# Attention scores of two components, issued in turn on the two halves of TensorE's rows

## The chip, the cores and the metric

The kernel runs on one core of one Trainium2 chip. The metric is the device time of one execution in microseconds (us); of three runs of the kernel before, the median is 1934.57 us (1925.41 to 1936.29).

## The reference

A backbone of two layers for 512 latent tokens and 256 context tokens of 1024 channels. Each layer has a modulated RMS norm, one input projection whose columns feed three groups of heads (a long convolution, a gated unit, differential attention), an output projection, and a SwiGLU feed-forward part. The change is in the differential attention alone: four heads, each with two components of 64 channels, whose softmaxes are subtracted:

```
s = einsum('bqhcd,bkhcd->bhcqk', q, k) * (DA_HEAD_DIM ** -0.5)
a = softmax(s, axis=-1)
w = a[:, :, 0] - lam * a[:, :, 1]
o = einsum('bhqk,bkhd->bqhd', w, v)
```

Latent queries attend to all 256 context keys and all 512 latent keys in one softmax. Context tokens attend to the 256 context keys, in layer 0 only, since nothing reads their result in layer 1.

## The kernel before, in words

All of TensorE's large products are computed from split operands: each float32 value is a high part of 12 bits and the exact rest, and a product is three matmuls, high by high, high by low and low by high. `mm3` (line 245) issues the three, on lines 251, 252 and 253, for every product in the kernel, so most of TensorE's time stands on these three lines; what a row is for is read from its shape. Scores are the only products on 64 rows whose output has 128 rows and comes from these lines.

`attend` (line 654) takes two heads. For each half of the query tokens, each head and each tile of 128 queries it computes the scores of component 0 and then of component 1. A head's 128 channels lie on the 128 partitions: component 0 on partitions 0 to 63, component 1 on 64 to 127, and so on the two halves of the array's rows. For a latent tile a component has 768 score columns, 512 latent and 256 context ones, in two PSUM banks: three matmuls of 512 columns, then three of 256. For a context tile it has 256 columns in one bank. After each component VectorE takes the row maximum (line 683) and scales it (line 686), and ScalarE takes the exponential out of PSUM and its sum (line 688). When both components have theirs, VectorE forms the weighted difference (lines 692 to 694). After two tiles the weights are transposed on TensorE (line 703), split, and multiplied with the values. There are 16 latent tiles in a layer and 8 context tiles.

PSUM has eight banks, which one arena hands out, the longest unused first (`Arena.get`, line 62). Scores take theirs from the group S, banks 2 to 5, by `ps` (line 219); the gated unit, the convolution and the filter spectra use the same group for some steps, and the latent stream's projections use S and A.

The work is written as generators, one per task: the latent stream, the context stream, the filter spectra and the modulation weights. `woven` (line 167) runs several side by side. Each step of a generator adds its matmul time to `self.cost` (columns / 2400 for each matmul), and the generator whose sum over its rate is lowest goes next; a step counts as at least 1. In `lat_mixer` (line 1416) the first pair of heads is woven with the gated unit and the projections of the second pair (line 1433), and the second pair with the output projection and the norm that follows it (lines 1442 to 1448). The order of issue is the priority with which a planner then puts each instruction on its engine's queue: an instruction whose operands or whose memory are not due yet by its plan lets later ones of other tasks go ahead. Each engine takes its queue in that order, and instructions wait there for semaphores.

Of the kernel before, what the change touches and what calls it, by code (L numbers as in the profile page):

```python
# [38 lines left out]
class Buf:  # L39
    """A piece of an arena; emit-time lifetime, slices like a tile."""  # L40
# [11 lines left out]
class Arena:  # L52
    """Blocks of one tile, handed out longest-unused first, so that reuse waits little."""
# [8 lines left out]
    def get(self, shape, allowed=None):  # L62
# [9 lines left out]
        for p in range(0, self.units - u + 1, step):  # L72
            if allowed is not None and p not in allowed:
                continue
            if any(self.used[p:p + u]):
                continue
            blk = p // 4 * 4
            whole = u < 4 and not any(self.used[blk:blk + 4])
            key = (whole and allowed is None, max(self.stamp[p:p + u]))
            if best is None or key < best[0]:  # L80
                best = (key, p)
# [12 lines left out]
    def fits(self, sizes):  # L94
        """Whether blocks of these units can be had, one beside the other."""
        used = list(self.used)
        for u in sorted(sizes, reverse=True):
            step = 4 if u > 2 else u
            p = next((p for p in range(0, self.units - u + 1, step) if not any(used[p:p + u])), None)
            if p is None:  # L100
                return False
            used[p:p + u] = [True] * u
        return True
# [9 lines left out]
class Stream:  # L113
    """One token stream (latent or context) in channel-major form."""
# [10 lines left out]
# PSUM banks by use, arena sizes in KiB per partition.  # L125
BANKS = {"A": (0, 1, 6, 7), "S": (2, 3, 4, 5), "W": (6, 7), "P": (6, 7)}
UNITS = {"R": 104, "RW": 24, "F": 44, "FW": 24}
# Rates of the tasks in each phase (the latent stream has 10), and of the woven steps of each layer.
# [5 lines left out]
# Work of the latent and of the context stream that GpSimd does ("mix": 2 is all of it, 1 a half).  # L134
# [8 lines left out]
# Steps of the tasks that come first, the chunks of modulation weights that are fetched ahead, and  # L143
# the arenas of the weights of the first feed-forward tiles.
# [5 lines left out]
class Net:  # L150
# [16 lines left out]
    def woven(self, *tasks):  # L167
        """Generators (gen, rate) side by side; the matrix work of each grows at its rate.

        A rate may be a key of self.rates, which change with the phases."""  # L170
# [20 lines left out]
    def room(self, *sizes):  # L191
        """Waits until the float32 arena has room for the next step."""
        while not self.F.fits(sizes):
            yield "wait"

    def claim(self, n):
        """Waits until n units of the operand arena are spoken for by nobody."""
# [25 lines left out]
    def tt(self, n, dtype=F32):  # L223
        """Tiny per-partition scratch, round robin."""
# [5 lines left out]
    def split(self, src, hi, lo, lo_eng=None):  # L230
        """hi = src rounded to 12 bits, lo = the rest, exactly."""
# [3 lines left out]
    def weights(self, src, *shape, pool=False, arena=None):  # L235
        """A split piece of weights of this shape; the low part by GpSimd if pool."""
# [8 lines left out]
    def mm3(self, out, terms):  # L245
        """out = sum of lhsT^T rhs over split terms: hi hi + hi lo + lo hi."""
# [9 lines left out]
    def rsqrt(self, ms, n, out=None):  # L256
        """1/sqrt by an exponent guess and three Newton steps."""
# [12 lines left out]
    def rstd_bcast(self, sq, T, n, groups="P", scale=None):  # L270
        """sq [P, T]: squares per channel row; PSUM [P, T] with 1/rms per token in every row.

        With scale [P, T / P] the channels are scale times the values that are meant: the result
        normalizes the values and takes the factor out."""
# [52 lines left out]
    def lambdas(self):  # L327
        """The weights of the second softmax, and the gains that follow."""
# [18 lines left out]
    def rope_tables(self, l):  # L347
        """Rotation tables of q and k with the norm gains folded in."""
# [10 lines left out]
    def ada_load(self, l, c, arena):  # L359
        """A chunk of modulation weights, as it is, in two pieces."""  # L360
# [6 lines left out]
    def ada(self, l, secs, groups="P", ready=(), own="W"):  # L367
        """Modulation sections; mods[l][:, s*8+k, v] is channel k*128+p of section s for stream v."""
# [60 lines left out]
    def x_open(self, st, a):  # L429
        """Channel tiles 2a and 2a+1 of x, resident or fetched from the home of the stream."""  # L430
# [12 lines left out]
    def pairs(self, n, T):  # L443
        """n split operands of [P, T]."""
        return [Pair.one(self.r(2, T)) for _ in range(n)]

    def square(self, st, k, x, cols=slice(None)):
        """Adds the squares of x, channel tile k, to the running sum; k in order."""
# [10 lines left out]
    def norm(self, st, l, w, cols=slice(None), squares=True, early=None):  # L459
        """st.h = split(rmsnorm(x) * G + shift), channel-major."""  # L460
# [37 lines left out]
    def modulate(self, st, l, w, k, y, cols):  # L498
        """y * G + shift in y's place and its high part; gives what makes the low part."""
# [15 lines left out]
    def proj_cm(self, st, l, n, out):  # L515
        """out [P, T]: the n-th 128 output channels of the input projection by tokens."""
# [4 lines left out]
    def proj_tm(self, st, w, tt, out):  # L521
        """out [P, 256]: one token tile by the chunk's 256 output channels."""
# [3 lines left out]
    def pool(self, st, i):  # L526
        """Whether GpSimd does this part of the stream's work."""
        return POOL[i][st.v]

    def win(self, st, l, c):  # L530
        """Weights of 256 output channels, in two pieces along the input channels."""
        return [self.weights(self.A["w_in_tm"][l, c - 4, :, 4 * i:4 * i + 4], 4, CW, pool=i and self.pool(st, "in tm")) for i in range(2)]

# [1 line left out]
    def qk(self, st, l, c, i, rope):  # L535
        """Two heads of q (i=0) or k (i=1): projection, norm per 64 channels, rotation;
        split [(component channel), tokens] per head."""
# [60 lines left out]
    def vproj(self, st, l, c):  # L598
        """Two heads of v, token-major: per two token tiles a split [P, 2, 256]."""
# [13 lines left out]
    def kqv(self, st, l, j, rope, q=True):  # L613
        """Keys, queries and values of heads 2j and 2j+1."""
# [27 lines left out]
    def kv_io(self, st, j, mem, store):  # L642
        """Keys and values of a head pair of a context-sized stream to or from DRAM scratch."""
# [9 lines left out]

    def attend(self, st, l, j, srcs):
        """Heads 2j and 2j+1 of stream st over the keys and values of srcs."""
# [8 lines left out]
        for qh in range(0, st.nt, 2):  # L664
# [3 lines left out]
            for h in range(2):  # L668
                q = st.q[j][h]
                ws = []  # L670
                for qt in (qh, qh + 1):
                    yield from self.room(e, e, 2)
                    i0 = 2 * h + qt - qh
                    es, sums = [], [s0[:, i0:i0 + 1], self.tt(1)]
                    for c in range(2):
                        b = self.ps("S", nk)
                        r = slice(c * HD, (c + 1) * HD)
                        off = 0
                        for s in reversed(srcs):
                            self.mm3(b[:, off:off + s.T], [(q[r, qt * P:(qt + 1) * P], s.k[j][h][r, :])])  # L680
                            off += s.T
                        m = self.tt(1)
                        nc.vector.tensor_reduce(m, b.ap, axis=AX.X, op=ALU.max)  # L683
# [4 lines left out]
                        nc.scalar.activation(es[c].ap, b.ap, AF.Exp, bias=m, scale=scale,  # L688
                                             accum_out=sums[c])
                        b.free()  # L690
# [115 lines left out]
    def sin_reduced(self, out, z, n):  # L806
        """out = sin(z) for any moderate z: z - 2 pi round(z / 2 pi) in three parts, then the table."""
# [22 lines left out]
    def dft(self, out, tab, cs, ft, data, n):  # L830
        """out[f, ch] = sum over tokens (one parity) of tab[token, f] * data[token, ch]."""
# [3 lines left out]
    def filters(self, groups="S"):  # L835
        """Hidden features of the filter networks: rows 64 l + channel, columns SEQ | CTX positions."""
# [33 lines left out]
    def spectra(self, l, L, dst, groups="S"):  # L870
        """Filter spectra of layer l at length L, scaled by 1/L, to DRAM scratch."""
# [76 lines left out]
    def short_conv(self, st, l, c, split_par):  # L948
        """Width-3 convolution of one 256-channel chunk; even|odd token order where asked."""
# [25 lines left out]
    def to_tokens(self, src, par, n, groups):  # L975
        """PSUM [P, n, 256]: one parity of [ch, even|odd tokens] with tokens on partitions."""
# [7 lines left out]
    def fwd(self, data, tabs, kdram, o, L, groups):  # L984
        """Spectral product of token-major data (per parity, split [P, n, 256]) with a filter.

        Gives split operands: even tokens take (cos, sin) = (a, c), odd tokens (b, d), each [P, n, 256]."""
# [140 lines left out]
    def outproj(self, st, l, ks, last=False):  # L1128
        """x += gate1 * (w_out[ks rows]^T mix[ks])."""
# [29 lines left out]
    def outproj_last(self, st, l, ks, parts):  # L1159
        """The last rows of the output projection, all columns, in parts of the tokens."""  # L1160
# [28 lines left out]
    def hidden(self, st, w, a, cols):  # L1189
        """a = split(silu(g) * u) for one tile of FFN channels and a range of tokens."""  # L1190
# [19 lines left out]
    def ffn(self, sts, l, rounds, ahead=(), last=False, ready=None):  # L1210
        """The feed-forward part of the streams, which share the weights.

        The first tiles, their weights in the arenas of ahead, take the tokens of the first stream
        in halves; only after them the other streams have to be ready."""
# [63 lines left out]
class Pair:  # L1278
    """Split operand: indexing gives the same piece of hi and lo."""
# [20 lines left out]
class Columns:  # L1300
    """Split weights [2, P, k, 128] of two tiles of output channels, in one piece or two.

    The second piece is fetched when the first is; a piece goes when it is done, unless on hold."""
# [259 lines left out]
def _layout(i):  # L1563
    """The inputs, only moved: transposed, cut into tiles, repeated."""
# [55 lines left out]
```

## Time and profile before

| | |
|---|---|
| median of 3 runs (lowest to highest) | 1934.57 us (1925.41 to 1936.29) |
| span of the profiled execution | 1924.6 us |
| the run nearest to that span | 1925.41 us |
| TensorE busy (matmul, weight load) | 1813.6 us, 1558.6 us |
| VectorE, ScalarE, GpSimd busy | 1082.6, 689.1, 119.7 us |
| granted TensorE clock, mean | 0.968 |

The span runs from the first to the last instruction of the core. PE is TensorE's matmuls, PEld its weight loads, DVE VectorE, ACT ScalarE, POOL GpSimd. Matmuls are pipelined: a row's start is when it began, its duration reaches into the next matmul's, so the pace is read from start to start. The granted clock is a share of full speed; the engine has two levels, 1.2 and 2.4 GHz.

### The profile page before, as it was taken

The numbers are of one execution on the slowest core, as the hardware profiler recorded it, in microseconds if no ns is written. First come the engines' busy times: TensorE is split into PE (matmuls) and PEld (weight loads), VectorE is DVE, ScalarE is ACT, GpSimd is POOL, SyncE is SP. The second block draws the span as 40 slices with busy tenths as digits, with TensorE's granted clock in tenths as the row PEclk, the third lists the DMA queues.
The fourth block names the chain that finished last, engine by engine and source line by source line (L and its number), as shares of the span: only waits on it lengthen the run. The fifth ranks groups of instructions, "written<-read, shape, count | busy, mean of one in ns | idle before, by whom it ended". The sixth has DMA issues, their size and how long they took to land.

```text
span 1924.6 us, 27933 instructions
## 1 busy us (share of the span) xinstructions
PE 1813.6 (94%) x11106; PEld 1558.6 (81%) x11106; DVE 1082.6 (56%) x2255; ACT 689.1 (36%) x1203; POOL 119.7 (6%) x128
## 2 busy tenths in 40 slices
PE   5799999789997999999999999899999999999999
PEld 2578898678776888888888888689988788888887
DVE  5677886778767523232423244789588773333333
ACT  2544434544544421212122112543455462222221
POOL 1100223211001000000000000011000000000000
PEclk9899899799997999999999999899999899999999
DMA  7567644235444343243424234444213222323231
GB/s 272 177 233 237 201 162 143 83 125 187 134 167 147 111 126 127 84 136 108 144 83 151 74 102 156 153 154 144 79 34 119 64 71 63 110 84 105 89 97 64
DMA packets 89564, 245.41 MB, mean 128 GB/s; under 512 B 9780, under 2 KB 21782, under 8 KB 89434
## 3 DMA queue, kind: packets, MB, share of 16 engines
q1 hardware_dynamic: 81162, 221.71, 35.2%
q0 software_dynamic: 8272, 21.92, 3.8%
q8 instruction: 87, 1.43, 0.3%
q14 instruction: 43, 0.35, 0.1%
HBM read 221.18 MB, written 22.41 MB: 127 GB/s over the span
## 4 chain that ended last, share of the span: by engine, by line
PE 79%; DVE 9%; DMA 4%; ACT 3%; issue 2%; POOL 0%; SPq 0%; ACTq 0%; DVEq 0%; POOLq 0%
PE banks L251 25%; PE banks L252 24%; PE banks L253 24%; PE banks L401 2%; PE banks L703 1%; DMA x_ctx<-F 1%; DVE RW L233 1%; DMA F<-x_ctx 1%; ACT F L688 1%; DVE tiny L683 1%; DVE F L1025 1%; PE banks L375 1%; PE banks L279 1%; DVE F L456 1%; DMA FW<-in_w_out 0%
## 5 line engine op out<-in xcount | busy, mean ns | idle before, releaser
L251 PE MATMUL banks<-R,RW 128*128 128x512 f32 (+1 forms) x1984 | 696.0, 352 | 9.1 <-ACT R L504 3.9
L252 PE MATMUL banks<-R,RW 128*128 128x512 f32 (+1 forms) x1984 | 693.9, 350 | 3.0 <-DVE R L507 3.0
L253 PE MATMUL banks<-R,RW 128*128 128x512 f32 (+1 forms) x1984 | 692.2, 349 | 0.5 <-DVE RW L233 0.5
L232 ACT ACTIVATE RW<-FW 128x1024 fp32r<-128x1024 f32 (+2 forms) x240 | 240.5, 1003 | 541.4 <-PE banks L252 418.9
L251 PEld LDWEIGHTS banks<-R,RW 128*128 128x128 f32 x1984 | 376.9, 190 | 64.7 <-ACT R L504 4.7
L252 PEld LDWEIGHTS banks<-R,RW 128*128 128x128 f32 x1984 | 377.0, 190 | 51.4 <-DVE R L507 3.8
L253 PEld LDWEIGHTS banks<-R,RW 128*128 128x128 f32 x1984 | 376.7, 190 | 50.4 <-issue 2.0
L233 DVE TENSOR_TENSOR RW<-FW,RW 128x1024 fp32r<-128x1024 f32 (+2 forms) x228 | 262.7, 1154 | 238.0 <-ACT RW L232 229.4
L1186 DVE SCALAR_TENSOR_TENSOR F<-banks,mods,F 128x512 f32<-128x512 f32 (+1 forms) x192 | 116.2, 615 | 177.4 <-PE banks L253 133.8
L251 PE MATMUL banks<-R 128*128 128x256 f32 (+3 forms) x584 | 188.0, 340 | 26.4 <-ACT R L1036 13.7
L252 PE MATMUL banks<-RW,R 128*128 128x256 f32 x624 | 180.0, 289 | 5.4 <-DVE RW L233 5.4
L251 PE MATMUL banks<-RW,R 128*128 128x256 f32 x624 | 181.1, 291 | 0.4 <-ACT F L552 0.2
L252 PE MATMUL banks<-R 128*128 128x256 f32 (+3 forms) x584 | 179.6, 319 | 1.4 <-DVE R L233 1.4
L253 PE MATMUL banks<-RW,R 128*128 128x256 f32 x624 | 180.2, 289 | 0.0
L253 PE MATMUL banks<-R 128*128 128x256 f32 (+3 forms) x584 | 177.5, 315 | 1.2 <-DVE R L1038 1.2
L251 PEld LDWEIGHTS banks<-R 128*128 128x128 f32 (+1 forms) x584 | 117.4, 209 | 49.6 <-ACT R L1036 15.2
L1204 DVE TENSOR_TENSOR F<-F,banks 128x256 f32<-128x256 f32 (+1 forms) x71 | 40.0, 565 | 208.5 <-PE banks L253 191.8
L232 ACT ACTIVATE R<-F 128x512 fp32r<-128x512 f32 (+1 forms) x133 | 72.0, 549 | 226.9 <-DVE F L1204 160.9
L252 PEld LDWEIGHTS banks<-R 128*128 128x128 f32 (+1 forms) x584 | 119.8, 209 | 10.0 <-issue 3.5
L252 PEld LDWEIGHTS banks<-RW,R 128*128 128x128 f32 x624 | 121.7, 195 | 7.6 <-DVE RW L233 6.3
L251 PEld LDWEIGHTS banks<-RW,R 128*128 128x128 f32 x624 | 121.5, 195 | 3.1 <-ACT F L552 0.8
L253 PEld LDWEIGHTS banks<-RW,R 128*128 128x128 f32 x624 | 121.8, 195 | 2.2 <-issue 1.5
(159 smaller groups left out, 1739.7 us busy)
## 6 DMA issues: line engine op xcount, KB each, us to landing
FW<-in_ffn_w SPq DMA_DIRECT2D x104, 512.0 KB, 3.7
FW<-in_ada_w SPq DMA_DIRECT2D x96, 512.0 KB, 5.0
FW<-in_w_in_tm SPq DMA_DIRECT2D x50, 512.0 KB, 4.8
R<-in_tab POOLq DMA_DIRECT2D x28, 512.0 KB, 4.9
FW<-in_w_in_cm SPq DMA_DIRECT2D x24, 512.0 KB, 4.7
F<-x_ctx SPq DMA_DIRECT2D x36, 256.0 KB, 3.6
FW<-in_ffn_w SPq DMA_DIRECT2D x24, 384.0 KB, 2.9
x_ctx<-F SPq DMA_DIRECT2D x32, 256.0 KB, 2.4
```

The lines of the kernel that those rows point to most:

```text
L232: self.nc.scalar.activation(hi, src, AF.Copy)
L233: (lo_eng or self.nc.vector).tensor_tensor(lo, src, hi.bitcast(F32), op=ALU.subtract)
L251: mm(out, lhsT=lh, rhs=rh, start=(i == 0), stop=False)
L252: mm(out, lhsT=lh, rhs=rl, start=False, stop=False)
L253: mm(out, lhsT=ll, rhs=rh, start=False, stop=(i == n - 1))
L279: nc.tensor.matmul(p1[:, t:t + 1], lhsT=sq[:, t * P:(t + 1) * P], rhs=self.ones[:, 0:1], start=True, stop=True)
L375: nc.tensor.matmul(pt[:, b], lhsT=sb[:, b // 2, b % 2 * P:(b % 2 + 1) * P], rhs=self.pick, start=True, stop=True)
L401: nc.tensor.matmul(pa[32 * j:32 * j + 32, :], lhsT=self.cv[:, 4 * i + j, :], rhs=w[:, j, :], start=(i == 0), stop=(i == 1), tile_position= ...
L456: nc.vector.tensor_tensor(st.acc[:, cols], st.acc[:, cols], q.ap, op=ALU.add)
L683: nc.vector.tensor_reduce(m, b.ap, axis=AX.X, op=ALU.max)
L1186: self.nc.vector.scalar_tensor_tensor(x, p, self.mods[l][:, sec * 8 + k, st.v:st.v + 1], x, op0=ALU.mult, op1=ALU.add)
L1204: nc.vector.tensor_tensor(s.ap, s.ap, u, op=ALU.mult)
```

## The change

`attend` takes one buffer for both components of a tile: four banks, always banks 2 to 5, for a latent tile, and two banks of group S for a context tile. A new function `scores` issues the matmuls of both components in turn: component 0 high by high, component 1 high by high, component 0 high by low, and so on, for the 512 latent columns and then for the 256 context columns. Maximum and exponential follow component by component as before, and the buffer is given back after both exponentials. `scores` adds 3 x columns / 2400 to `self.cost` once for both components. `Arena.get` gets an argument for a fixed place. The diff also empties comments and docstrings; this generates nothing and is left out here.

```
-    def get(self, shape, allowed=None):
+    def get(self, shape, allowed=None, at=None):
...
-        for p in range(0, self.units - u + 1, step):
+        for p in range(0, self.units - u + 1, step) if at is None else (at,):
...
+    def score_banks(self, nk):
+        if nk <= 512:
+            return self.B.get([P, 2, 512], set(BANKS["S"]))
+        return self.B.get([P, 2, 1024], at=BANKS["S"][0])
+
+    def scores(self, b, off, q, k, n):
+        (qh, ql), (kh, kl) = q, k[:, :]
+        self.cost += 3 * n / 2400
+        for i, (x, y) in enumerate(((qh, kh), (qh, kl), (ql, kh))):
+            for c in range(2):
+                r = slice(c * HD, (c + 1) * HD)
+                self.nc.tensor.matmul(b[:, c, off:off + n], lhsT=x[r], rhs=y[r], start=(i == 0), stop=(i == 2))
...
+                    b = self.score_banks(nk)
+                    off = 0
+                    for s in reversed(srcs):
+                        self.scores(b, off, q[:, qt * P:(qt + 1) * P], s.k[j][h], s.T)
+                        off += s.T
                     for c in range(2):
-                        b = self.ps("S", nk)
-                        r = slice(c * HD, (c + 1) * HD)
-                        off = 0
-                        for s in reversed(srcs):
-                            self.mm3(b[:, off:off + s.T], [(q[r, qt * P:(qt + 1) * P], s.k[j][h][r, :])])
-                            off += s.T
                         m = self.tt(1)
-                        nc.vector.tensor_reduce(m, b.ap, axis=AX.X, op=ALU.max)
+                        nc.vector.tensor_reduce(m, b[:, c, :nk], axis=AX.X, op=ALU.max)
...
-                        nc.scalar.activation(es[c].ap, b.ap, AF.Exp, bias=m, scale=scale,
+                        nc.scalar.activation(es[c].ap, b[:, c, :nk], AF.Exp, bias=m, scale=scale,
                                              accum_out=sums[c])
-                        b.free()
+                    b.free()
```

## Rows read from the trace of the kernel before

**Rows 1.** The page, parts 1 and 4: busy time, share, count; chain by engine.

```profile
PE 1813.6 (94%) x11106; PEld 1558.6 (81%) x11106; DVE 1082.6 (56%) x2255; ACT 689.1 (36%) x1203; POOL 119.7 (6%) x128
...
PE 79%; DVE 9%; DMA 4%; ACT 3%; issue 2%; POOL 0%; SPq 0%; ACTq 0%; DVEq 0%; POOLq 0%
```

**Rows 2.** Busy time by stretch: length, each engine (instructions), clock, DMA share, GB/s.

```profile
350.00:430.00 80.00, 67.30 (x413) 58.00 (x413) 61.31 (x138) 40.52 (x74) 18.35 (x14) 0.83 0.27 86
495.00:590.00 95.00, 86.50 (x554) 67.12 (x553) 67.34 (x156) 48.01 (x97) 0.57 (x1) 0.92 0.47 153
1378.00:1445.00 67.00, 66.89 (x451) 58.18 (x449) 57.08 (x145) 36.11 (x65) 0.00 (x0) 0.97 0.12 38
1445.00:1545.00 100.00, 93.39 (x531) 76.88 (x529) 80.24 (x200) 52.67 (x99) 1.65 (x3) 0.93 0.30 94
```

**Rows 3.** TensorE's timeline, 1436.0 to 1437.4: start, duration, line, shape.

```profile
1436.08 0.49 PE L251 MATMUL banks<-R 64*128 64x512 f32 x1
1436.41 0.39 PE L252 MATMUL banks<-R 64*128 64x512 f32 x1
1436.64 0.39 PE L253 MATMUL banks<-R 64*128 64x512 f32 x1
1436.87 0.28 PE L251 MATMUL banks<-R 64*128 64x256 f32 x1
1436.99 0.28 PE L252 MATMUL banks<-R 64*128 64x256 f32 x1
1437.11 0.28 PE L253 MATMUL banks<-R 64*128 64x256 f32 x1
1437.32 0.38 PE L253 MATMUL banks<-RW,R 128*128 128x256 f32 x1
```

**Rows 4.** TensorE's timeline, 1513.5 to 1515.5 (x2: two rows merged).

```profile
1513.57 0.49 PE L251 MATMUL banks<-R 64*128 64x512 f32 x1
...
1514.14 0.39 PE L253 MATMUL banks<-R 64*128 64x512 f32 x1
1514.15 0.51 PE L251 MATMUL banks<-R 64*128 64x512 f32 x2
...
1515.19 0.28 PE L253 MATMUL banks<-R 64*128 64x256 f32 x1
1515.40 0.39 PE L251 MATMUL banks<-R,RW 128*128 128x256 f32 x1
```

**Rows 5.** TensorE's timeline, 1462.5 to 1464.1.

```profile
1462.58 0.51 PE L251 MATMUL banks<-R 64*128 64x512 f32 x2
1462.92 0.40 PE L252 MATMUL banks<-R 64*128 64x512 f32 x2
...
1463.99 0.50 PE L251 MATMUL banks<-R,RW 128*128 128x512 f32 x1
```

**Rows 6.** TensorE's timeline, starts of two runs of twelve score matmuls.

```profile
351.74 0.79 PE L251 MATMUL banks<-R 64*128 64x512 f32 x1
...
1526.01 0.50 PE L251 MATMUL banks<-R 64*128 64x512 f32 x1 [2.52 <-ACT F L688]
```

**Rows 7.** The timeline of all engines, 1384.5 to 1386.7.

```profile
1384.58 0.99 ACT L688 ACTIVATE F<-banks,tiny,rq 128x768 f32<-128x768 f32 x1
...
1385.56 0.98 ACT L688 ACTIVATE F<-banks,tiny,rq 128x768 f32<-128x768 f32 x1
...
1386.68 0.50 PE L251 MATMUL banks<-R 64*128 64x512 f32 x1
```

**Rows 8.** VectorE's groups, 1378 to 1445: count, busy us, mean ns, idle before.

```profile
L683 DVE TENSOR_REDUCE tiny<-banks 128x1 f32<-128x768 f32 x16 | 15.2, 952 | 4.1 <-PE banks L253 4.1
L694 DVE SCALAR_TENSOR_TENSOR F<-F,tiny 128x768 f32<-128x768 f32 x7 | 7.1, 1013 | 0.0
...
L233 DVE TENSOR_TENSOR R<-banks,R 128x512 fp32r<-128x512 f32 x8 | 5.3, 686 | 1.9 <-ACT R L232 1.9
```

**Rows 9.** TensorE's waits, 350 to 430 and 1445 to 1545: total, times, longest.

```profile
PE banks L251 <- ACT F L688: 5.3, 2, 4.0
...
PE banks L251 <- ACT F L688: 2.5, 1, 2.5
```

## The prediction

> **What bounds the kernel now.** The order of reading was: the page's busy times and its chain of waits, then the busy time of each engine in the four stretches in which the latent stream attends, then TensorE's own timeline inside them, then its waits. TensorE is busy 94% of the span and carries 79% of the chain that ends last [rows 1], so a microsecond taken from its queue is worth most of a microsecond, as long as something else stands ready for it. The four attention stretches are less even [rows 2]. At 1378 to 1445 TensorE is busy 66.89 of 67 us, at 1445 to 1545 it is idle for 6.6 us, at 495 to 590 for 8.5 us, at 350 to 430 for 12.7 us, with a granted clock there of 0.83, that is, a third of the stretch at the lower of the two levels. VectorE is busy 77%, 71%, 85% and 80% of the four, in order of time. So TensorE sets the pace in one stretch of four, and in the others the softmax chain does so for part of the time.
>
> What the change touches is 32 latent tiles of scores (16 a layer), each two components of six matmuls on 64 rows: three of 512 columns and three of 256. TensorE's timeline shows three ways in which such a tile runs now. A component by itself takes 1437.32 - 1436.08 = 1.24 us [rows 3], so a tile whose components stand apart costs 2.48 us. Where the two components follow each other, the tile takes 1515.40 - 1513.57 = 1.83 us [rows 4]: the second component's first matmul (1514.15) starts 0.01 us after the third of the first component, while three of the first are still to come, and from there on the two run side by side on the two halves of the rows. In one tile both first matmuls start together and it takes 1463.99 - 1462.58 = 1.41 us [rows 5]. So the overlap that the change asks for is there already in part. Going through the timeline, the latent matmuls form fourteen unbroken runs of twelve with both halves (the first at 351.74, the last at 1526.01 [rows 6]), seven of them at 1.83 to 1.85 us; the rest, the equal of 18 tiles, is broken by work of other tasks or by waits.
>
> **The change part by part.** *Alternating order.* Nothing is added or removed: the same twelve matmuls and twelve weight loads a tile. Fully paired, a tile costs what one component costs now plus the step between the halves, an estimate of 1.24 + 0.01 = 1.25 us, or 1.41 us by the nearest row [rows 3, 5]; I take 1.25. An unbroken run then saves 1.83 - 1.25 = 0.58 us, a broken tile up to 2.48 - 1.25 = 1.23 us. The ceiling is 14 x 0.58 + 18 x 1.23 = 30.3 us, the floor nothing.
>
> Which tiles will pair? The planner puts an instruction on TensorE's queue when its operands and its bank are due. The first component's banks come free with its exponential, the second's 0.98 us later (1385.56 against 1384.58, and the next scores start only after them, at 1386.68) [rows 7]. A tile whose first component is due earlier will go on being issued first component first, whatever order the code has. So I let the fourteen unbroken runs pair, and 2 of the 18 broken ones. Of the fourteen, two stand in the stretch where TensorE is full and count whole; four at 1445 to 1545 and six at 495 to 590 count by half, since the idle time there shows that a TensorE that is earlier often waits for the softmax; two at 350 to 430 count nothing. That is 2 + 5 = 7 x 0.58 = 4.1 us, and 2 x 1.23 = 2.5 us for the broken ones. What comes late next is VectorE: its row maxima, weighted differences and low parts of the attention are 15.2 + 7.1 + 5.3 us of the full stretch [rows 8].
>
> That row stands beside a rule of the Trainium skill, TensorEngine Tiling (Array Packing), section PSUM Bottleneck: tiling speeds up the matmuls but not the emptying of PSUM, which can become the limit. Were it so in all four stretches the 4.1 us would be nothing; the trace agrees for three of them and not for 1378 to 1445, where TensorE has 0.1 us to spare and VectorE 9.9 us.
>
> *Context tiles* (8 in layer 0, three pairs of 256 columns): 24 matmuls on either half at 0.12 us from start to start (1436.99 - 1436.87 [rows 3]) are 2.9 us that could go beside the other half; I take 1 us, between nothing and 2.9.
>
> *The four-bank buffer.* Before, two components in two banks each also filled the four score banks, so the depth is the same. It adds no instruction. What it can add is a wait: the second matmul of a tile now belongs to the second component. Bounds: nothing, where both halves are free; 0.98 us a tile where the planner's order is ahead of the real exponentials [rows 7]. I take nothing, because TensorE's waits for the exponential are few now: 5.3 us in two waits and 2.5 us in one [rows 9], and the last of them, at 1526.01 [rows 6], holds up a first component, which either order does.
>
> *The weave.* The step of a latent tile was booked at 2 x 3 x 768 / 2400 = 1.92 and is now 0.96, which the weaver counts as 1. A head's two tiles and its product with the values were 3 x 1.92 = 5.76 and become 3.92, so beside one head's softmax stands 3.92 / 5.76 = 0.68 of the other tasks' matmuls. The softmax has the same work in less cover, and the uncovered matmuls run later, where TensorE is full. The price is idle TensorE. Bounds: if all stretches fell to the idle share of 350 to 430 (15.9%), the other three would lose 95 x 0.159 - 8.5 = 6.6, 67 x 0.159 - 0.1 = 10.6 and 100 x 0.159 - 6.6 = 9.3, together 26.5 us; in the other direction a new weave could at best fill the 27.9 us that are idle now [rows 2]. I take the one step that I can see coming: the full stretch falls to the idle share of the last one, 67 x 0.066 = 4.4 us lost.
>
> **Sum.** 4.1 + 2.5 + 1.0 - 4.4 = 3.2 us less. The profiled span is 1924.6 us and the nearest run 1925.41, 0.8 us around it: 1922.2 by that execution. It stands 9.2 us below the median of the three runs, 1934.57; on the median the forecast is 1931.4 us.
>
> **The rivals.** *All tiles pair.* For it: the code gives both components as one block, and halves that are both due can run as at 1462.58 [rows 5]. Against: the staggered release of the banks. Price: with the same shares (whole in the full stretch, half elsewhere), about two thirds of 30.3, 20 us less: 1915 us.
>
> The Trainium skill's page TensorE: Matmul & The Clock Gate, section The mechanism, has matmuls start and end in the order of the program, with no reordering. By that rule only an alternating order can pair, and what the change gives is near this rival's. The start at 1514.15 [rows 4] does not go with it, unless the planner had already mixed the two components.
>
> *The buffer blocks.* The second matmul of a tile waits for the second component's exponential, with the first component's other five and everything of the other tasks behind it in TensorE's queue. For it: the 0.98 us gap in rows 7. Against: the planner knows the banks. Price: 18 broken tiles x 0.98 = 17.6 us lost against 5.1 us gained, 12.5 us more: 1947 us. It decides once the waits of TensorE for the exponentials exceed some 20 us.
>
> *The thinner weave costs more than the pairing saves.* For it: three of four stretches idle already, and in one of them the clock is down to 0.83 [rows 2]. Against: later work may move up into the gaps. Price: between 4.4 and 26.5 us lost, against 7.6 us gained; at its middle 8 to 13 us more, 1943 to 1948 us; I take 1946 us.
>
> *It does not do what it says:* the planner keeps the components apart everywhere and only the weave changes: 1934.6 + 4.4 - 1 = 1938 us; I count it in the forecast's own range.
>
> **How the numbers follow.** Forecast 0.42, its own range 1922 to 1941 us; all tiles pair 0.22; thinner weave 0.23; blocked buffer 0.13. Some 0.5%, or 9.7 us, is what a measurement of this kernel tells from no change: faster is below 1924.9, slower above 1944.2. The forecast gives 0.12 faster, 0.25 same, 0.05 slower; all tiles pair 0.20 and 0.02 same; the thinner weave 0.07 same and 0.16 slower; the blocked buffer 0.04 same and 0.09 slower. Together 0.32, 0.38, 0.30. The range reaches beyond the paired rival's 1915 and the 1947 of the blocked one by the 7 us or so by which their prices are uncertain: 1908 to 1954 us.
>
> **What would show it.** Pairing: 512-column matmuls on 64 rows starting two at a time, 0.34 and then 0.23 us apart, and 1.25 to 1.41 us a tile; count of such tiles 14 to 16 (forecast) or above 25 (all pair). Weave: TensorE idle in the stretch that was full, and the last score tile of each stretch earlier against the work beside it. Blocked buffer: waits of 64-row matmuls for the exponential, one per tile. The forecast is wrong if the median lies outside 1922 to 1941 us, if more than 25 tiles pair, or if the waits for the exponentials grow by over 10 us.

## The result, and the profile after

The changed kernel takes 1960.97 us in the median of four runs (1959.34 to 1965.34); the kernel before, beside it, takes 1929.99 us (1925.08 to 1936.29). The ratio is 1.0154, with a 95% interval from 1.0123 to 1.0185: 31 us slower, and above the range of the prediction.

The profiled execution took 1962.23 us, with a span of 1960.5 us. Its page answers to [rows 1], first busy time and share by engine, then the chain that ended last.

```profile
PE 1829.7 (93%) x11106; PEld 1570.2 (80%) x11106; DVE 1079.4 (55%) x2255; ACT 689.0 (35%) x1203; POOL 118.3 (6%) x128
...
PE 22%; DVE 1%; ACT 0%; issue 0%; ACTq 0%
```

The same 11106 matmuls ran and TensorE was busy 16.1 us longer for them (1829.7 against 1813.6 us); its idle time grew by the other 19.8 us of the span's 35.9. (The chain of this profile breaks off after a quarter of the span, so its shares aren't used.)

The pairing itself came as described. In the profile after, scores are on line 667, the exponential on 702, the transposes on 717. TensorE's timeline of the changed kernel, where both components of a tile were due (start, duration, line, shape; x12 is the whole tile):

```profile
1407.26 1.31 PE L667 MATMUL banks<-R 64*128 64x512 f32 x12
1408.51 0.39 PE L251 MATMUL banks<-RW,R 128*128 128x256 f32 x1
```

The tile takes 1408.51 - 1407.26 = 1.25 us, against 1.83 us in [rows 4]. Of the 96 pairs of 512-column matmuls of the latent tiles, 34 start together, against 14 before. And yet the kernel is slower; where, a table by stage tells. Its boundaries are the starts and ends of the latent score tiles in each trace: the first head pair of layer 0 up to the start of the second pair, the second pair, from there to layer 1's attention, and layer 1's attention. First the kernel before (length, busy us of TensorE's matmuls, its weight loads, VectorE, ScalarE and GpSimd with their instructions, granted clock, DMA share, GB/s):

```profile
351.70:496.60 144.90, 126.64 (x888) 112.36 (x887) 111.56 (x271) 72.47 (x137) 26.09 (x18) 0.91 0.40 130
496.60:580.40 83.80, 80.81 (x513) 63.35 (x512) 58.24 (x133) 37.88 (x74) 0.57 (x1) 0.94 0.45 148
580.40:1379.60 799.20, 771.70 (x4814) 677.42 (x4812) 368.42 (x672) 230.57 (x378) 29.29 (x33) 0.98 0.38 124
1379.60:1539.90 160.30, 157.40 (x962) 133.11 (x962) 132.99 (x333) 83.28 (x156) 1.65 (x3) 0.96 0.23 71
524.50:545.00 20.50, 20.23 (x146) 15.35 (x145) 10.78 (x26) 6.30 (x11) 0.00 (x0) 1.00 0.52 168
```

The same stages of the changed kernel, then a piece of the second pair, and the stretch that was full before ([rows 2], its third row):

```profile
352.40:498.00 145.60, 124.47 (x818) 109.69 (x817) 96.15 (x233) 64.08 (x115) 24.68 (x18) 0.83 0.37 114
498.00:603.90 105.90, 97.91 (x557) 75.48 (x557) 66.87 (x154) 44.85 (x91) 0.00 (x0) 0.84 0.38 123
603.90:1407.30 803.40, 772.98 (x4842) 678.12 (x4840) 371.70 (x687) 233.01 (x382) 29.78 (x34) 0.98 0.39 125
1407.30:1572.20 164.90, 156.68 (x962) 133.80 (x962) 131.65 (x322) 82.47 (x157) 1.65 (x3) 0.93 0.23 69
524.50:545.00 20.50, 19.89 (x79) 15.02 (x80) 11.93 (x27) 9.56 (x20) 0.00 (x0) 0.50 0.26 77
1407.00:1475.00 68.00, 67.43 (x451) 59.38 (x451) 56.20 (x145) 34.57 (x65) 0.00 (x0) 0.95 0.13 37
```

Of the 35.9 us, 22.1 lie in the second head pair of layer 0 (105.9 against 83.8 us); 4.2 in the long stage behind it, 4.6 in layer 1's attention, 0.7 in the first pair, and the rest ahead of the first pair and after the attention. The small parts are within what a stage differs by from one execution to the next (last section). The 22.1 us are not: the second pair took 101.6 to 106.7 us in all five other profiles in which the first pair is booked at half and its rate left (e2, e3, w1, y1 and z1 below), and 80.9 to 85.3 us in e1, e5 and x1.

Three things fill the 22.1 us. The first pair was left with 70 matmuls fewer (888 to 818); 44 of them now stand in the second pair (513 to 557) and 28 after it. The 44 are mostly 18 of 512 columns (the latent output projection) and 24 of 256 (the context stream), together 60 blocks of 256 columns, or some 7 us at the 0.12 us from start to start that [rows 3] shows. Idle TensorE went from 83.80 - 80.81 = 3.0 to 105.90 - 97.91 = 8.0 us. And the records show TensorE at the lower of its two clock levels for 34.1 us of this stage, against 10.2: 23.9 us at 1.2 instead of 2.4 GHz, an estimated 12 us if matmuls set the pace throughout. The three make 24, a little more than 22.1, since some of the idle time lies at the lower level and is counted twice.

The moved work is a loss only because the first pair, rid of it, did not get shorter. That pair was at the lower level for 49.2 us, against 25.7, and idle for 145.60 - 124.47 = 21.1 us, against 18.3. Over both pairs together TensorE is busy 14.9 us longer for 26 matmuls fewer, and idle 7.9 us longer.

What TensorE did at that level, the groups of 524.5 to 545 show. Before (count, busy us, mean ns, idle before):

```profile
L251 PE MATMUL banks<-R,RW 128*128 128x512 f32 x16 | 6.5, 407 | 0.0
L252 PE MATMUL banks<-R,RW 128*128 128x512 f32 x16 | 6.4, 398 | 0.0
L253 PE MATMUL banks<-R,RW 128*128 128x512 f32 x16 | 6.3, 396 | 0.0
```

After, the same 20.5 us:

```profile
L667 PE MATMUL banks<-R 64*128 64x512 f32 x12 | 7.0, 721 | 0.0
L375 PE MATMUL banks<-pick,F 128*128 128x2 f32 x16 | 3.9, 357 | 2.6 <-DVE F L479 2.6
L717 PE MATMUL banks<-ident,F 128*128 128x128 f32 x12 | 3.6, 438 | 0.0
L667 PE MATMUL banks<-R 64*128 64x256 f32 x12 | 3.4, 412 | 0.0
L401 PE MATMUL banks<-FW,cv 128*32 128x256 f32 x16 | 1.9, 631 | 0.0
```

Before, 48 matmuls of 512 columns on all 128 rows and no scores stood there, and the granted clock was 1.00. After, there are none of the 48: what ran were scores on 64 rows, transposes, two-column and 32-wide matmuls, and at the end 11 matmuls of 256 columns on all rows. TensorE counts as busy for 19.89 of 20.5 us and was granted 0.50.

The mix need not be the cause. The stretch begins with the idle time in the second row: TensorE had run 512-column matmuls up to 522.5 us and then stood still for 2.6 us in front of a product of the modulation weights (line 375). In e3 below, a stretch at the lower level (515.3 to 535.8 us) began in the same place, behind 2.8 us of idle time on that line. In the changed kernel it ended at 545 us, as the 256-column matmuls on all rows ran. No run tells the idle time from the thin work behind it.

### The profile page after: what moved, and what is told of

It reads as the page before. It is cut to its first block, busy times and chain, and to the rows that moved or that the text cites. A ratio compares the mean times of both kernels' runs of the same rounds, so it can differ in the third digit from the quotient of the medians.

```text
span 1960.5 us, 27950 instructions
## 1 busy us (share of the span) xinstructions
PE 1829.7 (93%) x11106; PEld 1570.2 (80%) x11106; DVE 1079.4 (55%) x2255; ACT 689.0 (35%) x1203; POOL 118.3 (6%) x128
## 5 line engine op out<-in xcount | busy, mean ns | idle before, releaser
L251 PE MATMUL banks<-R,RW 128*128 128x512 f32 (+1 forms) x1984 | 698.9, 353 | 5.5 <-ACT R L504 4.9
L251 PEld LDWEIGHTS banks<-R,RW 128*128 128x128 f32 x1984 | 379.6, 192 | 64.9 <-issue 7.3
L253 PEld LDWEIGHTS banks<-R,RW 128*128 128x128 f32 x1984 | 379.0, 191 | 49.2 <-issue 1.6
L251 PE MATMUL banks<-RW,R 128*128 128x256 f32 x624 | 180.9, 291 | 2.1 <-ACT RW L232 2.1
L251 PE MATMUL banks<-R 128*128 128x256 f32 (+1 forms) x440 | 134.0, 314 | 26.6 <-ACT R L1050 13.8
L252 PE MATMUL banks<-R 128*128 128x256 f32 (+1 forms) x440 | 132.6, 306 | 3.4 <-DVE R L233 3.4
L253 PE MATMUL banks<-R 128*128 128x256 f32 (+1 forms) x440 | 129.9, 301 | 1.2 <-DVE R L1052 1.2
L251 PEld LDWEIGHTS banks<-RW,R 128*128 128x128 f32 x624 | 122.0, 196 | 4.7 <-ACT RW L232 2.3
L251 PEld LDWEIGHTS banks<-R 128*128 128x128 f32 x440 | 91.1, 211 | 35.4 <-ACT R L1050 15.4
L667 PE MATMUL banks<-R 64*128 64x256 f32 (+1 forms) x432 | 98.0, 412 | 12.6 <-ACT F L702 11.5
```

Source lines behind the costliest of these rows:

```text
L251: mm(out, lhsT=lh, rhs=rh, start=(i == 0), stop=False)
L252: mm(out, lhsT=lh, rhs=rl, start=False, stop=False)
L253: mm(out, lhsT=ll, rhs=rh, start=False, stop=(i == n - 1))
L667: self.nc.tensor.matmul(b[:, c, off:off + n], lhsT=x[r], rhs=y[r], start=(i == 0), stop=(i == 2))
```

## The experiments

Three theories could explain the loss. A, the thinner weave: the scores are booked at half their former cost, and that alone loses the time. B, the four-bank buffer: both components' banks have to be free before a tile starts. C, the alternating order itself. The median before was 1933 to 1934 us in every group of runs below; ratios are to it, with their 95% intervals.

**Undoing one part at a time.** Full booking in the changed kernel:

```diff
-        self.cost += 3 * n / 2400
+        self.cost += 6 * n / 2400
```

> The changed kernel with the booking of the scores put back to 1.92 a latent tile (6 x columns / 2400 in scores, both components counted); alternating order and four-bank buffer stay. Theory (the thinner weave is the loss): the stretch of the second pair in layer 0 is back near 85 us, TensorE's time at the lower clock falls from 233 to below 150 us, and the median lies at 1920 to 1932 us. Rival (the buffer or the order itself is the loss): above 1945 us. Rival (both): 1933 to 1945 us.

Measured: 1935.31 us, 1.0012 (0.9994 to 1.0030). One number gives the loss back. In microseconds this lies in the range of the rival "both"; as a ratio to the kernel before of the same group (1933.42 us) it is no loss that can be told from nothing. TensorE's time at the lower level fell to 180 us, not below 150.

The changed kernel, booking still half, with three matmuls of component 0 and then three of component 1 in place of the alternation:

```diff
-        for i, (x, y) in enumerate(((qh, kh), (qh, kl), (ql, kh))):
-            for c in range(2):
-                r = slice(c * HD, (c + 1) * HD)
+        for c in range(2):
+            r = slice(c * HD, (c + 1) * HD)
+            for i, (x, y) in enumerate(((qh, kh), (qh, kl), (ql, kh))):
```

> The changed kernel with the six matmuls of component 0 issued before the six of component 1; the four-bank buffer and the booking of 0.96 stay. Theory (the weave is the loss, pairing gains a few us): 1960 to 1972 us. Rival (alternation is the loss, because a second component's first matmul blocks the queue): 1925 to 1940 us.

Measured: 1949.23 us, 1.0078 (1.0053 to 1.0103). That is between the two ranges: the alternation costs here, and the rest of the loss stays. The edit is not what its text says. `scores` is called once for the 512 columns and once for the 256, so the six of component 0 are not all ahead of component 1's, and 28 of the 96 pairs still start together, against 34. It is a third order, not the old one.

The kernel before, with the half booking and nothing else:

```diff
                             self.mm3(b[:, off:off + s.T], ...)
+                            self.cost -= 1.5 * s.T / 2400
```

> The kernel before with nothing but the booking of the scores halved (1.5 x columns / 2400 taken back after each component's product). Theory (the weave alone makes the loss): 1955 to 1975 us, and the cold stretches of the changed kernel between 520 and 640 us return. Rival (buffer or order): 1925 to 1938 us, as before.

Measured: 1951.52 us, 1.0103 (1.0060 to 1.0146), a little under the theory's range and far from the rival's. The booking is no instruction, and it costs 18 us by the medians, 20 by the ratio.

The changed kernel with full booking and two buffers of two banks, as before:

```diff
-                    b = self.score_banks(nk)
+                    b = [self.ps("S", nk) for _ in range(2)]
```

> Alternating order alone: each component takes its own two banks from the arena as before, the booking is 1.92. Theory: within 4 us of the run with the four-bank buffer and the full booking, 1920 to 1932 us, as the buffer's depth is the same. Rival (fixed banks cost): 5 us or more below that run.

Measured: 1930.05 us, 0.9977 (0.9956 to 0.9997). So A holds, for 1.0 of the 1.5%; what the order does under the half booking is taken up below. At full booking alternating in own banks gains 0.2%, and the shared buffer seems to give it back (1935.31 against 1930.05 us, whose intervals overlap slightly, so the 0.3% for the buffer is likely, not shown).

The two pairs of layer 0 with the half booking alone (e3):

```profile
349.60:487.50 137.90, 120.39 (x816) 107.01 (x815) 99.18 (x233) 63.80 (x115) 25.66 (x18) 0.89 0.38 120
487.50:593.60 106.10, 99.78 (x557) 77.15 (x557) 67.15 (x154) 44.47 (x91) 0.00 (x0) 0.84 0.39 124
```

The second pair with full booking in the changed kernel (e1):

```profile
507.40:590.60 83.20, 78.67 (x511) 61.42 (x512) 58.37 (x133) 37.68 (x74) 0.57 (x1) 0.92 0.44 146
```

The half booking by itself brings the changed kernel's picture: 557 matmuls, 106.1 us, clock 0.84. Full booking brings back the old one for this pair: 511 matmuls, 83.2 us.

**Which stage, and whether more booking would be better still.** The half booking in the second pair of layer 0 alone, in the kernel before:

```diff
+                            self.cost -= 1.5 * s.T / 2400 if st.v == 0 and (l, j) == (0, 1) else 0
```

> The kernel before with the booking of the scores halved only for the second pair of heads of layer 0. With it halved everywhere the median was 1.0% above before, and the trace lost 15 us between 350 and 594 us, net of moved work, 5 in the feed-forward after it and 6 in layer 1. Theory (the loss sits in that stage, where attention runs out of cover and TensorE falls to the lower clock): 1.0055 to 1.0105 of before, 1944 to 1954 us, with a cold stretch of some 20 us at 510 to 540. Rival (the loss is spread over all four stages): below 1.004, under 1941 us.

Measured: 1933.05 us, 0.9997 (0.9977 to 1.0017). The stage in which the time shows is not the one in which it is lost: thinning its own cover did nothing.

One and a half times the booking, in the version with own banks:

```diff
-        self.cost += 6 * n / 2400
+        self.cost += 9 * n / 2400
```

> Alternating order with own banks, each latent tile booked at 2.88 in place of 1.92, so more of the other tasks' matmuls stand beside each tile. Theory (cover is what the attention stretches lack): fewer waits for the exponentials and 3 to 10 us below the same kernel at full booking, 1920 to 1927 us. Rival (the full booking is where the weave is best, either side loses): 5 us or more above it, 1935 us or more.

Measured: 1960.88 us, 1.0135 (1.0112 to 1.0158). Too much cover is as bad as too little. TensorE's waits in the first pair of this kernel (total, times, longest) give a likely reason: work that is woven in comes before its operands are ready. The first is a product of the gated unit. It waited for the split of the unit's normalised values (line 232, at 369.1 us), which waited for VectorE, and VectorE for a load; its weights had been split by 360.2 us. The second is a product of the modulation weights.

```profile
PE banks L251 <- ACT R L232: 14.8, 2, 14.3
PE banks L375 <- DVE F L479: 7.0, 1, 7.0
```

**Where the gain of the pairing goes.** In the first pair of layer 0 the waits for the exponential grew from 5.3 us [rows 9] to 7.7 + 5.1 = 12.8 us in the changed kernel, in part for a gate product (L251) that shares the score banks:

```profile
PE banks L251 <- ACT F L702: 7.7, 2, 5.6
PE banks L667 <- ACT F L702: 5.1, 2, 3.1
```

With own banks and full booking (e5) they were 12.8 us as well, so they come without the shared buffer too. That pair's row in e5 has the 888 matmuls of the kernel before and is 153.3 us long, against 144.9 (145.9 and 146.1 in y2 and x1 below, which run the kernel before's program up to there):

```profile
344.90:498.20 153.30, 130.04 (x888) 113.80 (x887) 112.90 (x271) 72.58 (x137) 25.10 (x18) 0.86 0.39 122
```

So in this one profile the alternation made the first pair longer. The gate was given other banks, with the alternation and without:

```diff
-        sg = net.sgu(lat, l)
+        sg = net.sgu(lat, l, "A")
```

> Alternating order with own banks and full booking; the latent gated unit's mixing products go to the banks of group A in place of S. In the run without this, TensorE waited 9.6 us at 345 to 498 and 1.7 us in layer 1 in line 251 for an exponential to give back a score bank. Theory (pairing's gain was handed back there): these waits go, 5 to 10 us less, 1920 to 1926 us, ratio 0.992 to 0.996. Rival (the softmax chain paces the stretch whatever waits): TensorE waits elsewhere, ratio 0.997 or more.

> The kernel before with the gated unit's mixing on group A, alone. Theory: the wait that goes is 4.0 us, so 0.997 to 1.000. If it gains as much as the same edit on the alternating order, the alternating order still has nothing to show for its matmul time.

Measured: 1931.65 us, 0.9985 (0.9970 to 0.9999), and 1934.53 us, 1.0003 (0.9987 to 1.0019). The gate's waits for the exponential went, and nothing was gained: others came in their place. TensorE's waits of the first of the two in the first pair:

```profile
PE banks L251 <- ACT R L1050: 5.6, 1, 5.6
PE banks L717 <- DVE F L809: 4.4, 2, 3.5
```

**The stages again.** Half booking in the kernel before for the first pair of layer 0 alone, and for layer 1 alone; the conditions are `(l, j) == (0, 0)` and `l == 1` in the line of x1.

> The kernel before with the booking of the scores halved only for the first pair of heads of layer 0. Halving it for the second pair alone changed nothing (ratio 0.9997), halving it everywhere 1.0103. Theory (the first pair's lighter booking lets the latent stream run ahead of the context stream, whose output projection, 60 blocks of 256 columns, moves into the second pair's stretch): that stretch grows from 84 to over 95 us, ratio 1.005 to 1.010. Rival (only all halvings together do it): below 1.003.

> The kernel before with the booking halved in layer 1 alone. With it halved everywhere, from the start of layer 1's attention to the end the trace took 550.6 us in place of 545.0. Theory: 1.001 to 1.004. Rival (layer 1 carries the loss): 1.006 or more.

Measured: 1943.76 us, 1.0042 (1.0023 to 1.0062), and 1929.43 us, 0.9985 (0.9960 to 1.0010). The first pair costs 0.4%, layer 1 nothing that can be measured. In the first of the two the second pair's stage took 101.6 us, as its theory had it, though the ratio is just under the theory's range. The text for it put all 60 blocks that moved down to the context stream; by their shapes 36 of them are the latent output projection.

Own banks, full booking, alternating in layer 1 only:

```diff
+        for i, (x, y), c in [(i, t, c) for i, t in terms for c in range(2)] if turns else [(i, t, c) for c in range(2) for i, t in terms]:
...
+                        self.scores(b, off, q[:, qt * P:(qt + 1) * P], s.k[j][h], s.T, l == 1)
```

> Own banks and full booking; component after component in layer 0, where alternating went with 12.8 to 17.2 us of waits for the exponentials in place of 5.3, and alternating in layer 1 only. Theory (alternation costs in layer 0's first pair and gains nothing elsewhere): 0.996 to 1.000, the layer 0 waits back near 5 us. Rival (pairing gains in layer 1): below 0.996. Rival (it gains in layer 0): 1.000 or more.

Measured: 1930.81 us, 0.9978 (0.9962 to 0.9994), the same as alternating everywhere. The waits for the exponential in layer 0's first pair were back at 4.3 + 1.0 = 5.3 us, and that gained nothing over e5. Layer 0 runs three by three here, as in e2, and 44 of the 96 pairs started together; so the run does not tell in which layer the 0.2% arise.

**VectorE's chain, and the booking of a layer.** If the softmax on VectorE eats the pairing's gain, a shorter softmax should free it. Both kernels leave out the weighted difference of the two components' weights (the second also alternates, in own banks with full booking):

```diff
-                    nc.vector.scalar_tensor_tensor(es[0].ap, es[1].ap, r, es[0].ap, op0=ALU.mult, op1=ALU.add)
```

> The kernel before without the weighted difference of the two softmaxes (line 694, 1.01 us of VectorE a latent tile; the first component's weights go on alone). It is the base for the next run. 32 x 1.01 us leave VectorE; 0.985 to 0.997 of before, as it is on the path in layer 0.

> Alternating order, own banks, full booking, and likewise without the weighted difference. Theory (VectorE's part of the softmax chain takes what pairing saves): with a shorter chain the gap to the run before it opens from 0.2% to 0.5 to 0.8%. Rival (the banks held until the exponential, or the order of the queue, take it): the gap stays at 0.0 to 0.3%.

Measured: 1905.47 us, 0.9855 (0.9826 to 0.9884), and 1917.98 us, 0.9913 (0.9884 to 0.9941). The intervals meet at 0.9884. With the shorter softmax alternating is not better by more than before but, by the medians, 0.6% worse: that theory fell.

Half booking for both pairs of layer 0, and for the first pair with its woven rate lowered to match:

```diff
-        ... woven((net.attend(lat, l, 0, [con, lat]), w[2]), ...)
+        ... woven((net.attend(lat, l, 0, [con, lat]), w[2] * (1 if l else 0.68)), ...)
```

> The kernel before with the booking halved for both pairs of layer 0. Theory (the loss is layer 0's, the two pairs together more than each alone): 1.006 to 1.010. Rival (each part adds what it costs alone): 1.002 to 1.005, and the 1.0% is made up of small losses in all four stretches.

> The kernel before with the booking halved for the first pair of layer 0 (ratio 1.0042 so far) and that pair's rate in its weave times 0.68, so that as many of the other tasks' matmuls stand beside a head's softmax as before. Theory (the loss is cover within that weave): 0.998 to 1.002. Rival (the loss is the latent stream's lead over the other streams, which this rate does not touch): 1.003 to 1.006.

Measured: 1948.99 us, 1.0085 (1.0057 to 1.0113), and 1934.81 us, 1.0006 (0.9978 to 1.0035). Layer 0 carries most of the 1.03%, and by the ratios its two pairs together lose more than the first alone (0.42%) and the second alone (nothing). By the medians the first pair's 0.42% come back when the attention's rate goes down by the factor that the prediction worked out, 0.68; the intervals of y1 and z3 overlap, so w2 below is the stronger case.

**The rest of the loss.** The changed kernel lost 1.5%, the half booking alone 1.0% in the old order. Open were the buffer and the order under half booking. Own banks with half booking, and the changed kernel, untouched but for its three attention rates:

```diff
-        yield from woven((net.attend(lat, l, 0, [con, lat]), w[2]), ...
+        yield from woven((net.attend(lat, l, 0, [con, lat]), 0.68 * w[2]), ...
```

> Alternating order with own banks at the halved booking: the changed kernel without its four-bank buffer. Theory (the order costs 0.5% under this booking, as its blocked matmuls have less cover): 1.013 to 1.017, like the changed kernel's 1.0154. Rival (the buffer costs it): 1.007 to 1.011, like the halved booking alone.

> The changed kernel with the rates of its latent attention in its own weaves times 0.68, in both layers; alternating order, four-bank buffer and halved booking stay. Theory (what the booking took is cover beside the tiles): 1.000 to 1.006, near the 1.0012 of the full booking. Rival (the latent stream's lead over the other streams carries the rest): 1.008 to 1.014.

Measured: 1954.00 us, 1.0116 (1.0062 to 1.0169), and 1938.95 us, 1.0025 (1.0004 to 1.0047). The first is too wide to tell the buffer from the order. The second mends 1.3 of the 1.5% with the buffer, the order and the half booking all in place. Its second pair:

```profile
495.90:587.40 91.50, 86.77 (x534) 66.20 (x535) 62.18 (x147) 42.31 (x87) 0.00 (x0) 0.94 0.41 131
```

534 matmuls, 91.5 us, clock 0.94: about halfway back in work, and all the way in clock.

What stays open is the difference between alternating and issuing three by three, under half booking and in the shared buffer: 1.0154 against 1.0078 (e2), intervals apart. The first pair of e2, below, was 6.8 us shorter than the changed kernel's in the one profile that each has, at a clock of 0.87 against 0.83. No run told why.

```profile
345.00:483.80 138.80, 122.03 (x816) 108.28 (x815) 95.41 (x233) 63.84 (x115) 24.93 (x18) 0.87 0.38 119
```

## Why the prediction was wrong

- **What bounds the kernel** was read rightly as far as it went: TensorE, with idle gaps beside the softmax. It saw the clock of 0.83 in [rows 2] and gave it no price. That was a gap: in the profiles with less cover, TensorE was not only idle for longer but had a lower clock for what stayed (0.84 against 0.94 in the second pair).
- **The weave is the first step that failed.** "I take the one step that I can see coming: the full stretch falls to the idle share of the last one, 67 x 0.066 = 4.4 us lost." The cause was named and its factor, 0.68, was right (z3 and w2 undo it by just that factor). Place and price were not. The full stretch stayed full (67.43 of 68 us busy). The loss lies in layer 0, where the first pair gives up 70 matmuls without getting shorter and the second gets 44 of them late: 22.1 us longer, by idle time 5, moved work 7 and the lower clock an estimated 12. The half booking alone costs 1951.52 - 1933.42 = 18.1 us by the medians, four times the 4.4.
- **The pairing's gain is the second, 4.1 + 2.5 + 1.0 us.** Forecast were 3.2 us less, and it became 31.0 us more; of these 34 us the weave's wrong price is 18.1 - 4.4 = 13.7. Most of the rest came with the alternation: under the booking that the change itself brought, the 7.6 us of gain were a loss, 31.0 - 18.1 = 12.9 us by the medians against e3 (0.5% by the ratios, intervals overlapping) and 0.8% against e2, which has the same buffer and booking (intervals apart). In the profiles it shows in layer 0's first pair, 145.6 us against 137.9 in e3 and 138.8 in e2. With the rates fitted, nearly all of the 1.5% is gone and this part with it (w2). Why the order costs more where there is less cover stays open.
- **The size of a pair was right:** a paired tile takes the 1.25 us that were forecast, and the 34 of 96 pairs are some 11 tiles, against the 14 to 16 expected. But even at full booking the gain, counted whole or half, is worth less: 1933.42 - 1930.05 = 3.4 us with own banks, and nothing that can be measured in the shared buffer. In layer 1's attention of e5, against the kernel before's fourth row above, TensorE is 8.2 us less busy and the stage 0.3 us shorter; idle time went from 2.9 to 10.8 us. The row of e5:

```profile
1382.50:1542.50 160.00, 149.21 (x963) 127.50 (x962) 134.03 (x333) 81.77 (x156) 1.65 (x3) 0.96 0.23 72
```

- **That "a TensorE that is earlier often waits for the softmax"** fits this row, and where one wait was removed another came (x3). Which link holds the pace isn't settled: taking 1 us a tile from VectorE did not help the pairing (y5 against y4).
- **The buffer at nothing:** no run refutes it; at full booking it costs 5.3 us by the medians of e1 and e5, whose intervals overlap. The waits for the exponential were not few any more. They grew by 7.5 us in the first pair and over the whole trace from 8.8 to 11.5 + 8.2 = 19.7 us, just over the 10 us of growth that the prediction named as a sign of being wrong; before and after (total, times, longest):

```profile
PE banks L251 <- ACT F L688: 8.8, 4, 4.0
...
PE banks L667 <- ACT F L702: 11.5, 7, 3.1
PE banks L251 <- ACT F L702: 8.2, 3, 5.6
```

They were 19.7 us in e5 as well, which has own banks, so by these profiles they go with the alternation and not with the shared buffer.

- **The rivals.** The thinner weave came true in kind: 18.1 us, above the middle of its own bounds (4.4 to 26.5 us). Its 1946 us fell short, since they counted on the 7.6 us that pairing did not give. Its price had been bounded by idle shares alone, in three stretches that left out the second half of the first pair. All tiles pair did not happen; the most was 50 of 96 (e5), and there it was worth 3.4 us, not 20.

The best version found is the alternation in own banks with the booking as it was (e5, or in layer 1 alone, y3): 0.2% below the kernel before.

## What to carry to other kernels

Where a schedule is balanced by booked costs and rates, a cheaper instruction should not be booked cheaper without fitting the rates again: half the booking cost 1.0%, one and a half times the booking 1.35%, and the instructions that were to gain gave 0.2%. When work moves out from beside a thin stage, price three things: the idle time, the place where the work lands, and the granted clock of what is left; and look for the loss also in the stage behind the one that was thinned, where it showed here. Before pairing matmuls, see whether their halves already overlap and what the stage waits for next.

## What the hardware showed that was not expected

Matmuls on the two halves of the rows overtook each other: in the kernel before, with component 0's six issued ahead of component 1's, the first of component 1 starts at 1514.15 us while three of component 0 are to come, the next at 1514.38 [rows 4]. About half of what pairing can save a tile was there already (2.48 - 1.83 of 2.48 - 1.25 us).

TensorE counted as busy for 97% of a stretch in which it was granted 0.50 (524.5 to 545, above). It ran 64-row scores, transposes and narrow matmuls there, behind 2.6 us of idle time.

And the clock of the same work differs between executions. From layer 1's attention on, the kernel before and y1 run the same order of matmuls. In y1's profile this stage was

```profile
1387.20:1557.10 169.90, 166.88 (x963) 140.92 (x962) 133.15 (x333) 83.37 (x156) 1.66 (x3) 0.89 0.22 67
```

169.9 us at a granted 0.89 against 160.3 us at 0.96 before. x1 and z3 had 169.8 and 169.9 us for it, z1 160.9. So one profile of a stage is worth no more than some 10 us, and only the timed ratios decide.
